# Narrow experts' products from loaded float32 weights on both column halves, and the sticks' sums in hi and lo parts

## The chip, the core and the metric

The kernel runs on one core of a Trainium2 chip. The metric is the device time of one execution in microseconds. In the names below PE is the matrix engine (TensorE), PEld its weight loads, DVE the vector engine, ACT the scalar engine, POOL GpSimd, and SP the sync engine, whose queue issues the large weight transfers.

## The reference

Two blocks of two layers each work on 256 tokens of width 1024 in float32. The first block has a retention layer, a dense layer, band attention and one layer with 8 experts, of which each token takes 2. The second block has two hybrid layers (stick-breaking attention, top-k attention, a gated recurrence) with an MLP behind each. The two places that matter here:

```python
# the experts: D_MODEL 1024, D_FF_EXPERT 3584, N_EXPERTS 8, TOP_K 2
for e in range(N_EXPERTS):
    y = y + gates[..., e:e + 1] * ((silu(xn @ w_gate[e]) * (xn @ w_up[e])) @ w_down[e])
...
# stick-breaking attention, six heads, blocks of 128 queries
log_1m = jnp.where(past, jax.nn.log_sigmoid(-z), 0.0)
later = lax.cumsum(log_1m, axis=3, reverse=True) - log_1m
a = jnp.exp(jnp.where(past, jax.nn.log_sigmoid(z) + later, NEG))
```

## The kernel before, in words

All weights are float32 in memory. PE multiplies "fp32r" operands, which keep fewer bits, so each float32 operand is cut in two: a high part (`whi`, a copy by ACT, L288) and a low part (`wlo`, the rest, by DVE, L289). A product is then three products of parts, hi·hi, lo·hi and hi·lo (`mm3`, L343 to L345).

The class `Stream` (L228 to L307) brings the weights. It holds a list of items in the order of use, each a tile of 128 partitions x 2048 float32, 1 MB. `fill` issues the transfer of the next items as long as a buffer is free; `_split` cuts the next half item into `whi` and `wlo` and frees the buffer when its second half is done; `get` hands out the parts that a product needs and lets `_split` run up to 5 half items (`HL`) ahead. There are 4 raw buffers (`RAW`), and 7 more (`widen`, pools raw3 and raw4) from the end of the attention layer to the last item of the last expert. SP issues the transfers in the order of the items, and each waits there for its buffer.

An expert is 42 items: for each of 14 blocks `j` of 256 hidden features two items of gate and up weights (`eu`) and one of down weights (`ed`). The eight experts are sorted by their load. Those in turns 0, 2, 3, 5 and 6 are wide (`WIDE`, L31): up to 128 slots, `mm3`. Those in turns 1, 4 and 7 are narrow: at most 64 slots. A narrow expert puts the high parts of its 64 tokens in columns 0 to 63 of the array and the low parts in columns 64 to 127 (`gather`, L977), so that two products, with `whi` (L1033) and with `wlo` (L1034), do all that is needed; a multiplication by `fold` (L1069), two identity matrices one above the other, adds both halves while it transposes.

In each block PE does the up products (`mm`), then the down products (`acc`) of the block before, then the transposes (`tp`); ACT and DVE do silu and the multiplication behind it (`split`, L1073, L1074). After the last block `acc` is cut into `yh` and `yl`, multiplied by the transposed one-hot matrix `ohT` (L1112) and added to `h` by DVE (L1114). The order on each engine comes from a scheduler, which is why work of two experts stands mixed where they meet.

`stick_breaking` (L1415) computes the sums over later keys as a product with a triangular matrix of ones (`c["later"]`), in float32, with four products of 128 columns for each of the two heads of a pair (L1443 to L1446); there are three pairs in each of two layers.

Of the kernel before, what the change touches and what calls it, by code (L numbers as in the profile page):

```python
# [23 lines left out]
KD = D // P  # L24
# [203 lines left out]
class Stream:  # L228


    def __init__(self, prog, plans, raw_bufs, hl_bufs, raw_pool, hl_pool):
        self.nc = prog.nc
        self.items, self.parts, self.first = [], [], []
        for ap, plan in plans:
            offs, _ = offsets(plan)
            for c, o in zip(plan, offs):
                self.first.append(len(self.parts))
                step = max(c.kt // 2, 1)
                self.parts += [(len(self.items), k, step) for k in range(0, c.kt, step)]
# [3 lines left out]
        self.free = {raw_pool: raw_bufs}  # L243
        self.base, self.extra = raw_pool, []
# [4 lines left out]
    def widen(self, pool, bufs, until):  # L249

        self.extra.append(pool)
        self.free[pool] = bufs
        self.last = next(i for i, it in enumerate(self.items) if it[1].key == until)
        self.fill()

    def fill(self, most=None):
        while self.n_raw < min(len(self.items), most or len(self.items)):
            pool = next((p for p in self.extra if self.n_raw <= self.last and self.free[p]), self.base)
            if not self.free[pool]:
                return  # L260
            ap, c, o = self.items[self.n_raw]
            f = c.kt * c.n
            t = pool.tile([P, 2048], F32, name="wraw")
            if c.key[0] in ("eu", "ed"):
                e = self.expert[c.key[1]] if c.key[1] else 0
                src = ap[e:e + 1] if isinstance(e, int) else ap[bass.ds(e, 1)]
                self.nc.sync.dma_start(t[:, :f], src[:, o:o + P * f].rearrange("o (p f) -> (o p) f", p=P))
            else:
                step = f if self.n_raw else f // 2
                for c0 in range(0, f, step):  # L270
                    self.nc.sync.dma_start(t[:, c0:c0 + step],
                                           bass.AP(tensor=ap.tensor, offset=ap.offset + o + c0, ap=[[f, P], [1, step]]))
            self.free[pool] -= 1
            self.raw[self.n_raw] = t, pool
            self.n_raw += 1

    def _split(self):
# [3 lines left out]
        t, pool = self.raw[i]  # L281
# [3 lines left out]
        for i0 in range(0, f, f // n):  # L285
            h, l = (x[:, i0:i0 + f // n] for x in (hi, lo))
            src = t[:, k * c.n + i0:k * c.n + i0 + f // n]
            self.nc.scalar.activation(h, src, AF.Copy)  # L288
            self.nc.vector.tensor_tensor(l, src, h.bitcast(F32), op=ALU.subtract)  # L289
        if k + nk == c.kt:  # L290
            self.free[pool] += 1
            del self.raw[i]
        self.hl[self.n_hl] = [x[:, :f].rearrange("p (k n) -> p k n", n=c.n) for x in (hi, lo)]
        self.n_hl += 1
        self.fill()

    def get(self, *keys):

        at = self.first[self.n_get]
# [3 lines left out]
        end = self.first[self.n_get]  # L303
        while self.n_hl < min(max(end, at + self.hl_bufs), len(self.parts)):
# [1328 lines left out]
```

## Time and profile before

| what | value |
| --- | --- |
| median of 3 runs | 2431.45 us (2431.17 to 2432.93) |
| the profiled execution's own time | 2430.9 us |
| its span, first to last instruction | 2429.1 us |
| busy: PE, PEld, DVE, ACT | 98%, 81%, 78%, 65% of the span |
| the eight experts | about 564 to 1536 us of the span |
| weights of the experts | 336 transfers of 1 MB |

The shares are means over stages with different limits. Matrix products overlap in PE's pipeline, so that a product's own duration is longer than the distance between the starts of two of them; PE's rate is read from starts. A plain float32 product stands in the trace as two records.

### The profile page before, as it was taken

The numbers are of one execution on the slowest core, as the hardware profiler recorded it, in microseconds if no ns is written. First come the engines' busy times: TensorE is split into PE (matmuls) and PEld (weight loads), VectorE is DVE, ScalarE is ACT, GpSimd is POOL, SyncE is SP. The second block draws the span as 40 slices with busy tenths as digits, with TensorE's granted clock in tenths as the row PEclk, the third lists the DMA queues.
The fourth block names the chain that finished last, engine by engine and source line by source line (L and its number), as shares of the span: only waits on it lengthen the run. The fifth ranks groups of instructions, "written<-read, shape, count | busy, mean of one in ns | idle before, by whom it ended". The sixth has DMA issues, their size and how long they took to land. (4 is left out here: it accounts for less than half of the span.)

```text
span 2429.1 us, 35661 instructions
## 1 busy us (share of the span) xinstructions
PE 2372.9 (98%) x13033; PEld 1968.2 (81%) x13033; DVE 1891.5 (78%) x3027; ACT 1568.7 (65%) x2609; POOL 60.5 (2%) x105
## 2 busy tenths in 40 slices
PE   8999999999999999999999999899999999999999
PEld 7978998888876787876788876698789889878898
DVE  6756567778989989899998899778775567877655
ACT  6446555667878777778777789645755554575554
POOL 0000000000000000000000000100000000100000
PEclk9999999999999999999999999899999999999999
DMA  7445555567989998999999999534345554434552
GB/s 289 169 161 209 190 191 191 203 239 283 368 327 399 360 366 330 356 356 413 345 366 345 367 359 381 148 134 160 137 165 203 188 168 145 169 128 173 191 191 105
DMA packets 88121, 605.20 MB, mean 249 GB/s; under 512 B 10456, under 2 KB 12128, under 8 KB 17024
## 3 DMA queue, kind: packets, MB, share of 16 engines
q1 hardware_dynamic: 85520, 593.39, 65.5%
q0 software_dynamic: 2416, 9.44, 1.8%
q8 instruction: 104, 1.70, 0.3%
q14 instruction: 81, 0.66, 0.1%
HBM read 601.74 MB, written 1.05 MB: 248 GB/s over the span
## 5 line engine op out<-in xcount | busy, mean ns | idle before, releaser
L289 DVE TENSOR_TENSOR wlo<-wraw,whi 128x512 fp32r<-128x512 f32 (+1 forms) x1656 | 1383.5, 876 | 369.6 <-ACT whi L288 351.7
L288 ACT ACTIVATE whi<-wraw 128x512 fp32r<-128x512 f32 (+1 forms) x1656 | 1204.1, 776 | 437.0 <-PE mm L344 191.6
L343 PE MATMUL mm<-xth,whi 128*128 128x256 f32 x1296 | 364.0, 281 | 0.0
L345 PE MATMUL mm<-xth,wlo 128*128 128x256 f32 x1296 | 361.7, 279 | 1.5 <-DVE wlo L289 1.5
L344 PE MATMUL mm<-xtl,whi 128*128 128x256 f32 x1296 | 361.8, 279 | 0.0
L344 PEld LDWEIGHTS mm<-xtl,whi 128*128 128x128 f32 x1296 | 245.5, 189 | 3.9 <-issue 2.1
L343 PEld LDWEIGHTS mm<-xth,whi 128*128 128x128 f32 x1296 | 243.5, 188 | 5.2 <-issue 3.0
L344 PE MATMUL acc<-wlo,hh 128*128 128x512 f32 x624 | 247.2, 396 | 0.0
L345 PE MATMUL acc<-whi,hl 128*128 128x512 f32 x624 | 246.6, 396 | 0.0
L345 PEld LDWEIGHTS mm<-xth,wlo 128*128 128x128 f32 x1296 | 243.6, 188 | 2.4 <-DVE wlo L289 1.7
L343 PE MATMUL acc<-whi,hh 128*128 128x512 f32 x624 | 235.3, 397 | 1.3 <-ACT hh L348 1.3
L343 PE MATMUL mm<-whi,xth 128*128 128x512 f32 (+2 forms) x592 | 231.3, 391 | 2.0 <-ACT whi L288 2.0
L344 PE MATMUL mm<-wlo,xth 128*128 128x512 f32 (+2 forms) x592 | 231.5, 391 | 0.3 <-DVE wlo L289 0.3
L345 PE MATMUL mm<-whi,xtl 128*128 128x512 f32 (+2 forms) x592 | 229.6, 388 | 0.5 <-DVE xtl L349 0.5
L343 PE MATMUL mm<-whi,xgh 128*128 128x512 f32 x560 | 224.9, 402 | 2.7 <-ACT whi L288 2.6
L344 PE MATMUL mm<-wlo,xgh 128*128 128x512 f32 x560 | 223.0, 398 | 3.1 <-DVE wlo L289 3.0
L345 PE MATMUL mm<-whi,xgl 128*128 128x512 f32 x560 | 221.4, 395 | 0.0
L1034 PE MATMUL mm<-wlo,xgh 128*128 128x512 f32 x336 | 143.3, 427 | 5.4 <-DVE wlo L289 4.5
L343 PEld LDWEIGHTS acc<-whi,hh 128*128 128x128 f32 x624 | 117.5, 188 | 28.9 <-ACT hh L348 3.2
L345 PEld LDWEIGHTS acc<-whi,hl 128*128 128x128 f32 x624 | 117.3, 188 | 28.2 <-DVE hl L349 0.5
L344 PEld LDWEIGHTS acc<-wlo,hh 128*128 128x128 f32 x624 | 117.4, 188 | 26.4 <-DVE wlo L289 0.3
L1033 PE MATMUL mm<-whi,xgh 128*128 128x512 f32 x336 | 134.2, 400 | 0.0
(394 smaller groups left out, 3098.0 us busy)
## 6 DMA issues: line engine op xcount, KB each, us to landing
wraw<-in_we_dram SPq DMA_DIRECT2D x336, 1024.0 KB, 6.1
wraw<-in_w_dram SPq DMA_DIRECT2D x218, 1024.0 KB, 4.8
wraw<-in_w_dram SPq DMA_DIRECT2D x4, 912.0 KB, 4.6
wraw<-in_w_dram SPq DMA_DIRECT2D x6, 512.0 KB, 3.6
bias<-in_rel_rows_dram POOLq DMA_DIRECT2D x4, 768.0 KB, 4.6
gain<-in_norm_ffn_dram POOLq DMA_DIRECT2D x2, 512.0 KB, 7.1
gn<-in_ret_gn_dram SPq DMA_DIRECT2D x4, 256.0 KB, 3.8
gain<-in_norm_ple_dram POOLq DMA_DIRECT2D x2, 512.0 KB, 5.9
```

What stands on the lines that cost most here:

```text
L288: self.nc.scalar.activation(h, src, AF.Copy)
L289: self.nc.vector.tensor_tensor(l, src, h.bitcast(F32), op=ALU.subtract)
L343: mm(out, l[0], r[0], start=start, stop=False)
L344: mm(out, l[0], r[1], start=False, stop=False)
L345: mm(out, l[1], r[0], start=False, stop=stop)
L1033: nc.tensor.matmul(out, x[0], wk[0], start=start, stop=False)
L1034: nc.tensor.matmul(out, x[0], wk[1], start=False, stop=stop)
```

## The change

In narrow experts the weights are no longer cut. `Stream.get` hands out the raw float32 tile itself, keeps its buffer until the next `get`, and only then frees it. Raw buffers are now parts of one tile for each pool, handed out from one list. The 64 tokens stay float32 (`xn`), and `halves` multiplies them as the array's stationary operand of 64 columns, once into partitions 0 to 63 with the left half of the weights' columns and once into 64 to 127 with the right half. The gate half and the up half of a block so land in the two partition halves of one bank with 256 columns, and the two halves of the model width in one bank with 512. Two plain transposes take the place of the fold; silu and the multiplication give the float32 `hn`, which isn't cut either. At the end one `yh` and one `yl` hold both halves, and the products with `ohT` take 64 rows each. Wide experts are as before. For the sticks' sums the triangle is stored as fp32r, the operand is cut in hi and lo parts, and each part takes one product of 384 columns and one of 128.

```diff
 class Stream:
+        self.plain = lambda c: c.key[0] in ("eu", "ed") and c.key[1] in plain
...
+    def room(self, pool, n, last):
+        t = pool.tile([P, n, 2048], F32, name="wraw")
+        self.last[id(t)] = last
+        self.free += [(t, k) for k in range(n)]
...
+    def release(self, i):
+        self.free.append(self.raw.pop(i))
+        self.fill()
...
     def get(self, *keys):
-        at = self.first[self.n_get]
+        for i in self.held:
+            self.release(i)
+        self.held = []
...
-        while self.n_hl < min(max(end, at + self.hl_bufs), len(self.parts)):
+        while self.n_hl < min(max(end, at + self.hl_bufs), len(self.parts)) \
+                and (self.n_hl < end or self.parts[self.n_hl][0] in self.raw):
             self._split()
+        if not self.plain(self.items[start][1]):
+            return [[x[:, k, :] for x in self.hl[i]] for i in range(at, end) for k in range(self.parts[i][2])]
+        self.held = list(range(start, self.n_get))
+        return [[t[:, a, k * c.n:(k + 1) * c.n]] for i in self.held
+                for (t, a), c in [(self.raw[i], self.items[i][1])] for k in range(c.kt)]
...
+    def halves(self, out, xs, ws, first, last):
+        m, width = None, out.shape[1]
+        for i, (x, (w,)) in enumerate(zip(xs, ws)):
+            for n in range(2):
+                before = [m] if m else []
+                m = self.nc.tensor.matmul(out[64 * n:64 * n + 64], x, w[:, n * width:(n + 1) * width],
+                                          start=first and i == 0, stop=last and i == len(xs) - 1)
+                self.after(m, before)
+        return m
...
+            def up(ps, k0, wu):
                 if wide[e]:
-                    self.mm3(out, x, wk, start, stop)
+                    for k in range(4):
+                        self.mm3(ps, [a[:, k0 + k, :] for a in xg], wu[k], k0 + k == 0, k0 + k == KD - 1)
                 else:
-                    nc.tensor.matmul(out, x[0], wk[0], start=start, stop=False)
-                    nc.tensor.matmul(out, x[0], wk[1], start=False, stop=stop)
+                    self.halves(ps[:, :256], [xg[:, k0 + k, :] for k in range(4)], wu, k0 == 0, k0 + 4 == KD)
...
+                if not wide[e]:
+                    if rows:
+                        ends.append(self.halves(acc[0], [hT[j][:, k, :] for j, k, _ in rows], [wk for *_, wk in rows],
+                                                 rows[0][:2] == (0, 0), rows[-1][:2] == (nj - 1, 1)))
+                    return
...
-                    for c in range(4):
-                        nc.tensor.matmul(tp[:, c], cp[:, c * P:(c + 1) * P], self.fold, start=True, stop=True)
+                    for k in range(2):
+                        self.after(nc.tensor.transpose(tp[:, k], cp[:, k * P:(k + 1) * P], self.ident), ends[-1:])
...
-                        nc.vector.tensor_tensor(sg, sg, tp[:, 2:], op=ALU.mult)
-                        self.split_psum(hh[:, :, :64], hh[:, :, 64:], sg)
+                        nc.vector.tensor_tensor(hT[j], sg, tp[:, :, 64:], op=ALU.mult)
...
-                nc.tensor.matmul(ps[:, 0:128], c["later"][:, 0], a[:, hh, 0:128], start=True, stop=True)
-                nc.tensor.matmul(ps[:, 128:256], c["later"][:, 0], a[:, hh, 128:256], start=True, stop=False)
-                nc.tensor.matmul(ps[:, 128:256], c["later"][:, 1], a[:, hh, 256:384], start=False, stop=True)
-                nc.tensor.matmul(ps[:, 256:384], c["later"][:, 0], a[:, hh, 256:384], start=True, stop=True)
+                parts = [pool.tile([P, 384], F32R, name="sah"), self.work.tile([P, 384], F32R, name="sal", tag="xs", bufs=3)]
+                self.split_psum(*parts, a[:, hh])
+                for x, w1, start, stop in ((0, 0, True, False), (0, 1, False, False), (1, 1, False, False), (1, 0, False, True)):
+                    if w1:
+                        nc.tensor.matmul(ps[:, 128:256], c["later"][:, 1], parts[x][:, 256:384], start=start, stop=stop)
+                    else:
+                        nc.tensor.matmul(ps[:, :384], c["later"][:, 0], parts[x], start=start, stop=stop)
```

How the order of instructions moves, at three places. First PE in a block of the narrow expert in turn 1. Before (`whi` and `wlo` are the cut weights, `xgh` the tokens' parts, `hh` the hidden features; "waits DVE" is the wait for a `wlo`, or in an `acc` row for `hh`):

```order
L1034 MATMUL mm<-wlo,xgh 128x512 [waits DVE_49]
L1033 MATMUL mm<-whi,xgh 128x512
L1034 MATMUL mm<-wlo,xgh 128x512
L1033 MATMUL mm<-whi,xgh 128x512 [waits Activation_49]
...
L1033 MATMUL acc<-whi,hh 128x512 [waits DVE_49]
L1034 MATMUL acc<-wlo,hh 128x512
...
L1069 MATMUL tp<-fold,cp 128x64 [waits Activation_49]
L1069 MATMUL tp<-fold,cp 128x64 x3
```

The same block now (`wraw` is the loaded tile; 64x256 and 64x512 are the outputs in one half of the array):

```order
L1048 MATMUL mm<-wraw,xn 64x256 [waits DMAHW2_49,PE_49]
L1048 MATMUL mm<-wraw,xn 64x256 x7
L1048 MATMUL mm<-wraw,xn 64x256 [waits DMAHW3_49]
L1048 MATMUL mm<-wraw,xn 64x256 x7
L1048 MATMUL acc<-wraw,hn 64x512 [waits DMAHW4_49,DVE_49]
L1048 MATMUL acc<-wraw,hn 64x512 x3
L1108 MATMUL tp<-ident,cp 128x128 [waits Activation_49]
L1108 MATMUL tp<-ident,cp 128x128
```

PE waited for DVE's parts of the weights; now it waits for each transfer itself.

Second, DVE where turn 1 (narrow) meets turn 2 (wide). Before (`sgn` and `hh` are the narrow expert's last hidden features, `yl` its output's low part, `h` the sum, the `wlo` rows from the second on belong to turn 2):

```order
L1074 TENSOR_TENSOR sgn<-sgn,tp 128x128 [waits Activation_49]
L289 TENSOR_TENSOR wlo<-wraw,whi 128x1024 [waits DMAHW7_49,Activation_49]
L349 TENSOR_TENSOR hh<-sgn,hh 128x2x64 [waits Activation_49]
L289 TENSOR_TENSOR wlo<-wraw,whi 128x1024 [waits Activation_49]
L289 TENSOR_TENSOR wlo<-wraw,whi 128x1024 [waits DMAHW0_49,Activation_49]
L349 TENSOR_TENSOR yl<-acc,yh 128x512 [waits Activation_49]
L289 TENSOR_TENSOR wlo<-wraw,whi 128x1024 [waits PE_49,Activation_49]
L1114 SCALAR_TENSOR_TENSOR h<-ps,in_turn,h 128x512 [waits PE_49] x2
```

Now:

```order
L1113 TENSOR_TENSOR hn<-sgn,tp 128x128 [waits DVE_49,Activation_49] x12
L368 TENSOR_TENSOR yl<-acc,yh 128x512 [waits Activation_49]
L1142 SCALAR_TENSOR_TENSOR h<-ps,in_turn,h 128x512 [waits PE_49]
L300 TENSOR_TENSOR wlo<-wraw,whi 128x1024 [waits DMAHW7_49,Activation_49]
L300 TENSOR_TENSOR wlo<-wraw,whi 128x1024 [waits Activation_49]
L1142 SCALAR_TENSOR_TENSOR h<-ps,in_turn,h 128x512 [waits PE_49] x3
L300 TENSOR_TENSOR wlo<-wraw,whi 128x1024 [waits DMAHW0_49,Activation_49]
```

The first low parts of the wide expert stood among the narrow expert's last steps; now they stand behind its output.

Third, SP's issues of expert weights in turn 1. Before, and below it now:

```order
L267 DMA wraw<-in_we_dram 128x2048 [waits DMAHW6_49,DVE_49]
L267 ISA
L267 DMA wraw<-in_we_dram 128x2048 [waits DMAHW7_49,DVE_49]
L267 ISA
L267 DMA wraw<-in_we_dram 128x2048 [waits DMAHW0_49,DVE_49]
```

```order
L275 DMA wraw<-in_we_dram 128x2048 [waits DMAHW6_49,DVE_49]
L275 ISA
L275 DMA wraw<-in_we_dram 128x2048 [waits DMAHW7_49,DVE_49]
L275 ISA
L275 DMA wraw<-in_we_dram 128x2048 [waits DMAHW0_49,PE_49]
```

From the item on whose buffer a narrow expert's weights held, the transfer waits for PE's products in place of DVE's low part.

## Rows read from the trace of the kernel before

**Rows 1.** The page's first line.
```profile
span 2429.1 us, 35661 instructions
```

**Rows 2.** Busy time by stage: from:to, length, engines (instructions), PEclk, DMA share, GB/s.
```profile
686.60:800.70 114.10, 101.53 (x465) 76.89 (x462) 106.73 (x119) 96.74 (x130) 0.00 (x0) 0.99 0.94 371
800.70:1054.00 253.30, 251.19 (x1122) 202.75 (x1123) 226.17 (x250) 187.92 (x235) 0.00 (x0) 0.99 0.93 352
1054.00:1166.00 112.00, 106.40 (x487) 76.26 (x485) 107.18 (x119) 96.38 (x130) 0.00 (x0) 1.00 0.98 391
1415.60:1533.10 117.50, 111.25 (x475) 73.67 (x472) 116.66 (x214) 107.15 (x222) 0.00 (x0) 0.99 0.84 330
1130.00:1166.00 36.00, 33.63 (x162) 24.24 (x160) 34.77 (x39) 32.16 (x44) 0.00 (x0) 1.00 1.01 416
```

**Rows 3.** Groups by line in turn 1, 686.6 to 800.7: busy, mean ns.
```profile
L289 DVE TENSOR_TENSOR wlo<-wraw,whi 128x1024 fp32r<-128x1024 f32 x84 | 98.9, 1220 | 2.5 <-ACT whi L288 1.8 <-PE tp L1069 0.7
L288 ACT ACTIVATE whi<-wraw 128x1024 fp32r<-128x1024 f32 x85 | 85.0, 1051 | 9.1 <-PE acc L1033 6.3 <-PE mm L1033 2.4 <-PE acc L345 0.3
```

**Rows 4.** Line L1034 (narrow, low parts): what PE sat idle for, us, times.
```profile
  DVE wlo L289: 61.4, 170
```

**Rows 5.** Timeline of PE in turn 1: start, length, line, idle before.
```profile
737.58 1.00 PE L1069 MATMUL tp<-fold,cp 128*128 128x64 f32 x8
...
738.70 0.39 PE L1033 MATMUL mm<-whi,xgh 128*128 128x512 f32 x1
738.93 0.40 PE L1034 MATMUL mm<-wlo,xgh 128*128 128x512 f32 x1
...
743.66 0.50 PE L1033 MATMUL acc<-whi,hh 128*128 128x512 f32 x1 [1.35 <-DVE hh L349]
```

**Rows 6.** Issues of weights by SP: start, length, count.
```profile
508.68 0.33 SPq L267 DMA_DIRECT2D wraw<-in_we_dram  x1
...
510.52 36.33 SPq L267 DMA_DIRECT2D wraw<-in_we_dram  x10
...
551.29 129.38 SPq L267 DMA_DIRECT2D wraw<-in_we_dram  x42
```

**Rows 7.** Transfers: count, KB each, median us from issue to landing.
```profile
wraw<-in_we_dram SPq DMA_DIRECT2D x336, 1024.0 KB, 6.1
```

**Rows 8.** Timeline of PE in the sticks' sums, float32 on the whole array.
```profile
1707.97 0.39 PE L1445 MATMUL sb<-sa,c_later 128*128 128x128 f32 x2
1708.19 0.39 PE L1446 MATMUL sb<-sa,c_later 128*128 128x128 f32 x2
```

**Rows 9.** Attention's float32 products on both column halves: the line's durations (ns), and a timeline.
```profile
L800 PE MATMUL po<-eT,v x96: 272/273/323, 472.0 to 527.6; 128*64 128x128 f32 x96
...
471.96 0.88 PE L800 MATMUL po<-eT,v 128*64 128x128 f32 x12
...
472.77 0.31 PEld L793 LDWEIGHTS pt<-ident,s 128*128 128x128 f32 x3 [0.17 <-issue]
```

**Rows 10.** Timeline where turn 1 meets turn 2.
```profile
802.18 0.60 ACT L348 ACTIVATE yh<-acc 128x512 fp32r<-128x512 f32 x1 [0.50 <-PE acc L1034]
...
803.04 0.68 DVE L349 TENSOR_TENSOR yl<-acc,yh 128x512 fp32r<-128x512 f32 x1
...
804.75 0.62 PE L1112 MATMUL ps<-yl,ohT 128*128 128x512 f32 x2
...
805.83 1.41 DVE L1114 SCALAR_TENSOR_TENSOR h<-ps,in_turn,h 128x512 f32<-128x512 f32 x2
```

**Rows 11.** Groups by line, 1000 to 1600 us: a wide block's steps behind the up products.
```profile
L1053 DVE TENSOR_TENSOR sg<-sg,mm 128x256 f32<-128x256 f32 x34 | 14.3, 420 | 2.9 <-ACT sg L1052 2.9
L1052 ACT ACTIVATE sg<-mm 128x256 f32<-128x256 f32 x34 | 13.1, 386 | 40.9 <-PE mm L345 40.9
```

**Rows 12.** The sticks: the step behind the sums (ns), and a stage with them (columns as rows 2).
```profile
L1447 DVE TENSOR_TENSOR zm<-zm,sb x12: 545/550/556, 1708.6 to 2162.7; 128x384 f32<-128x384 f32 x12
...
1680.00:1720.00 40.00, 38.62 (x215) 30.29 (x214) 31.86 (x77) 24.47 (x50) 0.00 (x0) 1.00 0.33 121
```

More of the change, by code (lines that the diff above doesn't have):

```diff
@@ L237, in __init__ @@
                 self.first.append(len(self.parts))
-                step = max(c.kt // 2, 1)
-                self.parts += [(len(self.items), k, step) for k in range(0, c.kt, step)]
+                if not self.plain(c):
+                    step = max(c.kt // 2, 1)
+                    self.parts += [(len(self.items), k, step) for k in range(0, c.kt, step)]
                 self.items.append((ap, c, o))
@@ L242, in __init__ @@
         self.first.append(len(self.parts))
-        self.free = {raw_pool: raw_bufs}
-        self.base, self.extra = raw_pool, []
+        self.free, self.last, self.held = [], {}, []
         self.hl_pool, self.hl_bufs = hl_pool, hl_bufs
@@ L247, in __init__, with widen @@
         self.n_raw = self.n_hl = self.n_get = 0
[L249 to L253, printed above, removed]
+        self.room(raw_pool, raw_bufs, len(self.items))
+    def room(self, pool, n, last):
+        t = pool.tile([P, n, 2048], F32, name="wraw")
+        self.last[id(t)] = last
+        self.free += [(t, k) for k in range(n)]
+    def widen(self, pool, n, until):
+        self.room(pool, n, 1 + next(i for i, it in enumerate(self.items) if it[1].key == until))
         self.fill()
@@ L257, in fill @@
         while self.n_raw < min(len(self.items), most or len(self.items)):
-            pool = next((p for p in self.extra if self.n_raw <= self.last and self.free[p]), self.base)
-            if not self.free[pool]:
+            place = next((p for p in self.free if self.n_raw < self.last[id(p[0])]), None)
+            if place is None:
                 return
+            self.free.remove(place)
+            t, at = place
             ap, c, o = self.items[self.n_raw]
             f = c.kt * c.n
-            t = pool.tile([P, 2048], F32, name="wraw")
             if c.key[0] in ("eu", "ed"):
@@ L280, in _split @@
         self.fill()
[L281 removed]
+        t, at = self.raw[i]
         f = nk * c.n
@@ L302, in get @@
             self.n_get += 1
-        end = self.first[self.n_get]
-        while self.n_hl < min(max(end, at + self.hl_bufs), len(self.parts)):
+        at, end = self.first[start], self.first[self.n_get]
+        self.fill()
+        while self.n_hl < min(max(end, at + self.hl_bufs), len(self.parts)) \
+                and (self.n_hl < end or self.parts[self.n_hl][0] in self.raw):
             self._split()
-        return [[x[:, k, :] for x in self.hl[i]] for i in range(at, end) for k in range(self.parts[i][2])]
+        if not self.plain(self.items[start][1]):
[3 more added lines that the diff above has]
+                for (t, a), c in [(self.raw[i], self.items[i][1])] for k in range(c.kt)]
 class Program:
@@ L522, in run @@
                                    (io["w2"], plan_second())], self.RAW, self.HL,
-                            raw_pool, hl_pool)
+                            raw_pool, hl_pool, [i for i in range(NE) if not WIDE[i]])
             self.h = self.keep.tile([P, NB, D], F32, name="h")
@@ L1086, in experts @@
                         split = None
-                    for k in range(4):
-                        product(ps, [a[:, k0 + k, :] for a in xg], wu[k],
-                                k0 + k == 0, k0 + k == KD - 1)
+                    up(ps, k0, wu)
                 rows = rows_of(j - 1) if 0 < j < nj - 1 else []
@@ L1170, in second_constants @@
         c = {}
-        for n in ("causal", "past_add", "past", "later", "rope", "levels"):
+        for n in ("causal", "past_add", "past", "rope", "levels"):
             c[n] = pool.tile(list(self.io[n].shape), I32 if n == "levels" else F32, name="c_" + n)
             self.nc.sync.dma_start(c[n], self.io[n])
+        ones = self.work.tile([P, 2, P], F32, name="ones", tag="xs", bufs=3)
+        self.nc.sync.dma_start(ones, self.io["later"])
+        c["later"] = pool.tile([P, 2, P], F32R, name="c_later")
+        self.nc.vector.tensor_copy(c["later"], ones)
         return c
```

99 lines of the change are left out of this document (56 added, 43 removed).

## The prediction, made before the changed kernel ran

> **What bounds the kernel now.** I began with the span [rows 1] and cut it into the experts' stages by the busy times per stretch [rows 2], since shares of the whole span mix stages with different limits. The narrow experts take 114.1 us (turn 1), 112.0 us (turn 4) and 117.5 us (turn 7, up to its last down product); two wide ones together 253.3 us, 126.6 us each. In the wide stages PE is busy for 251.2 of 253.3 us: they are bound by PE. In turn 1 DVE is busy for 106.7 of 114.1 us, 94%, and in turn 7 for 116.7 of 117.5 us, while PE has gaps of 12.6 and 6 us. The groups by line say with what: 84 low parts of 1220 ns are 98.9 us of DVE, the high parts 85.0 us of ACT [rows 3]. The waits before the products with low parts agree: 61.4 us over the three narrow experts [rows 4]. So narrow experts are bound by the cutting of weights, and the change takes that away whole.
>
> What is next must then be found. There are two candidates, both in these rows: the transfers, 42 items of 1 MB for an expert [rows 7], and PE with the new products.
>
> **The transfers.** With their engines full (share 1.01) they moved 416 GB/s in the stretch from 1130 us [rows 2]. An item of 1.0486 MB takes 2.52 us at that rate, an expert 105.9 us. But a narrow expert starts with buffers full. Up to 551 us 11 items had been issued and 42 more by 686.6 us [rows 6]; turn 0 used 42, so 11 of turn 1 were on their way or landed when it began. Left are 31 x 2.52 = 78.1 us. I add 3.7 us until the first buffer is freed, since its products stand mixed with 16 leftover products of turn 0 (16 x 0.23 us [rows 5]), 1.5 us for the last landing (an estimate, a quarter of the 6.1 us of rows 7, as its issue lies before) and 1.8 us of products behind it (below): 85.1 us.
>
> The Trainium skill, "DMA: Bandwidth & Descriptors", section "Specifications", gives a core about 358 GB/s from HBM. By that an expert would need 123 us and no narrow one could become shorter than it is. The measured 416 GB/s over 36 us [rows 2] decides against it; a milder form stays as a rival below.
>
> **PE's new products.** Float32 on the whole array: two records for 128 columns, the next pair 0.22 us later [rows 8], so 0.11 us a record; an fp32r product of 512 columns is 0.23 us behind the one before [rows 5]. Float32 thus costs four times as much per column. What pays for it is that the two column halves work side by side. The trace has such products: in attention 12 records of 128 columns, alternating between the halves, stand within 0.88 us, and the last one lasts 0.27 us, so 11 steps take 0.61 us, 0.055 us each, half of 0.11 [rows 8, 9]. With the number of columns a record costs 0.11 us at 256 and 0.22 us at 512. A block has 16 up products, 32 records, 3.55 us, and 4 down products, 8 records, 1.78 us. The fold of 1.00 us [rows 5], 8 records, becomes two transposes of a record each, 0.25 us. Twice a block the array changes between halves and whole; behind the products on halves a weight load stood 0.17 us without cause [rows 9], so 0.3 us. That is 5.88 us, 82.3 us for 14 blocks. At the end silu and the multiplication lie open, at most 0.39 + 0.42 us as in a wide block [rows 11], and the last down products, 0.9 us: 84.0 us.
>
> The Trainium skill, "TensorEngine Tiling (Array Packing)", section "Key Properties", says that changing the tiling mode drains the engine. This is the rule that speaks against the change. The 0.17 us agree with it in kind; the sum above has them, and a larger price is a rival.
>
> Both limits lie near 85 us. They overlap, not add: PE eats the 11 items of lead, then waits for transfers in the last blocks. I take 85 us.
>
> **Silu, copies, `hn`.** The copy of 256 columns, silu and one multiplication remain on ACT and DVE, both now nearly idle, under the 3.55 us of the next up products: nothing. If that cover went, they would cost at most the 0.39 + 0.42 us of the wide form [rows 11] in 14 blocks, 11 us.
>
> **Where a narrow expert meets a wide one.** Before, the wide expert's low parts were made ahead. Now DVE has them behind `yl` and a sum into `h`, and ACT has the high parts behind `yh` (the second place of the order). So behind the last down product come `yh` 0.60, `yl` 0.68, products with `ohT` 0.62, one sum 0.70, one low part 1.22 [rows 3, 10], with four hand-overs of 0.3 us (`yh` ends at 802.78, `yl` starts at 803.04) 5.0 us. In the first wide block only four half items are cut ahead, and ACT goes on only after that block's silu and `hh`: silu 0.39, multiplication 0.42, transposes 0.25, `hh` 0.39 (a copy of the same size as silu), a high part 1.05 and a low part 1.22 [rows 3, 11] are 3.7 us; with hand-overs I take 4 us. Both hold for turns 1 and 4. What waits behind these instructions on DVE and ACT is the wide expert's own cutting, and PE for it.
>
> **The sum for the experts.** To the point where PE runs through again a narrow expert takes 85 + 5 + 4 = 94 us. Before, that point was the stage's length plus 3.7 us of leftover products (16 x 0.23). Turn 1: 117.8 - 94 = 23.8. Turn 4: 115.7 - 94 = 21.7. Turn 7 has no wide expert behind it: 117.5 - 85 = 32.5, less 3 us because all four sums into `h` now stand at the end: 29.5. Together 75.0 us.
>
> Does the lead come back before turns 4 and 7? Wide experts use an item in 126.6 / 42 = 3.01 us, transfers bring one in 2.52 us. Over 84 items this is 41 us, 16 items, more than the 11 buffers: yes. For wide experts that start with empty buffers I take off 4.5 us in all, a high and a low part (2.27 us) for each of turns 2 and 5; it lies between 0 and twice that.
>
> **The sticks.** For each of 12 heads four products of 0.22 us become 2 x 0.17 + 2 x 0.06 us: 5.2 us of PE less. Added for each are a copy of 384 columns (about 0.5 us, from 0.60 for 512) and a subtraction (0.55 us, as the step of the same size in rows 12) in a chain. In such a stage PE is busy for 38.6 of 40 us with other products and ACT for 24.5 [rows 12], so the chain is mostly covered. Bounds: 5 us gained to 12 us lost; I take 2 us gained, near the busy PE.
>
> In the profiled execution, 2430.9 us with 2429.1 us of span, this is 75.0 - 4.5 + 2 = 72.5 us: 2358.4 us. The median is 0.55 us above that execution; I forecast **2359 us**.
>
> **Rivals.**
>
> *The transfers don't hold 416 GB/s in the long run.* Over whole stages they moved 352 to 391 GB/s [rows 2]. For it: turn 1's share of 0.94 at 371 is not far from full. Against it: in wide stages PE asks for no more. At 371 GB/s an item takes 2.83 us; turn 1 is 31 x 2.83 + 6.2 + 9 = 103, 15 us won; the wide experts refill 84 x 0.18 / 2.83 = 5 items, so turn 4 takes 37 x 2.83 + 15 = 120 and turn 7 about 114: 4 lost, 3 won. That is some 14 us, 2417 us.
>
> *Changing the array's mode costs more.* At 1 us each instead of 0.15 a block takes 7.6 us, an expert 108: with 9 us behind it turns 1 and 4 win nothing, turn 7 some 7 us, 2426 us. At 0.5 us a block is 6.6 us, an expert 94, 9 us more than forecast in each of three, 2386 us. Against it: the 0.17 us.
>
> *The halves don't overlap at 256 and 512 columns, the other side.* The overlap is seen at 128 columns alone. One after the other a block is 32 x 0.11 x 2 + 8 x 0.22 x 2 + 0.5 = 11 us, an expert 156, 42 us more than now, and with the meetings above some 140 us lost: 2570 us. It decides from a block of 8 us, about what one takes now (114.1 / 14). Against it: nothing in rows 9 depends on the length of a stream, and a longer one hides the weight loads better.
>
> *Nothing moves, because another wait sits right behind DVE's.* For it: ACT has 96.7 of 114.1 us of work in turn 1. Against it: most of that is the 85.0 us of high parts, which go too.
>
> **How the numbers follow.** My forecast, with the transfers and PE near 85 us, gets 0.80; its own range is 2343 to 2376: below, each narrow expert is 5 us shorter (boundaries better covered); above, the lead isn't quite full and the sticks lose. A sagging rate gets 0.07, a dear change of mode 0.07 (half of it near 2386), no overlap 0.04, nothing moved 0.02. The range for 8 in 10 reaches to the milder form of the mode's price and of the rate: 2338 to 2398 us. Two runs of this kernel can be told apart from about 0.2%, 5 us. Faster by more: 0.94, the forecast and the first two rivals; within it 0.02; slower 0.04.
>
> **What would show it.** Right: no cut weights in turns 1, 4 and 7; records of 64 output rows some 0.11 us (up) and 0.22 us (down) apart; blocks of 5.9 us at first and, in the last blocks, PE idle on `wraw` transfers; a transfer share near 1.0 at about 415 GB/s through turn 1 and the wide experts after it; a gap of some 5 us at the start of turns 2 and 5. Wrong: blocks over 8 us, transfers that stay below 390 GB/s with their share at 1, or turn 4 much longer than turn 1.

## The result and the profile after

| | median, us | range | runs |
|---|---|---|---|
| before | 2431.31 | 2430.47 to 2432.93 | 4 |
| changed | 2403.78 | 2400.02 to 2407.41 | 4 |

The ratio is 0.988, with a 95% interval of 0.987 to 0.990. The kernel became 27.5 us faster where 72.5 were forecast; 2404 us lies outside the forecast's range of 2338 to 2398. The profiled execution of the changed kernel took 2407.41 us, 3.6 us above the median, so differences of stages below are good to some 4 us.

The page's first line:

```profile
span 2405.6 us, 35418 instructions
```

Busy time by stage in the changed kernel (columns as in [rows 2]). The first four rows answer to rows of it: turn 1, turns 2 and 3, turn 4 and turn 7. The others are short stretches that the text comes to.

```profile
690.70:782.50 91.80, 88.53 (x609) 45.90 (x608) 8.56 (x21) 10.85 (x31) 0.00 (x0) 1.00 0.89 366
782.50:1046.60 264.10, 254.79 (x1109) 201.76 (x1109) 225.79 (x247) 186.35 (x232) 0.00 (x0) 0.97 0.92 370
1046.60:1140.80 94.20, 91.68 (x641) 48.31 (x640) 11.12 (x26) 13.45 (x35) 0.00 (x0) 1.00 0.91 370
1399.60:1491.70 92.10, 88.58 (x609) 45.91 (x608) 8.55 (x21) 10.85 (x31) 0.00 (x0) 1.00 0.95 387
1491.70:1523.50 31.80, 5.81 (x25) 4.06 (x25) 13.42 (x21) 9.43 (x20) 5.26 (x10) 0.58 0.80 206
690.00:695.00 5.00, 5.00 (x25) 3.45 (x24) 1.12 (x2) 1.17 (x3) 0.00 (x0) 1.00 0.00 0
695.00:700.00 5.00, 5.00 (x24) 2.28 (x24) 2.33 (x4) 0.41 (x1) 0.00 (x0) 1.00 0.21 49
720.00:760.00 40.00, 40.00 (x298) 21.07 (x296) 2.02 (x7) 4.63 (x14) 0.00 (x0) 1.00 1.01 421
770.00:800.00 30.00, 23.82 (x107) 13.33 (x108) 8.71 (x11) 5.43 (x8) 0.00 (x0) 0.89 0.51 199
```

In turn 1 DVE fell from 106.7 to 8.6 us and ACT from 96.7 to 10.9 us: the cutting is gone, as the change says. The stages are 18 to 25 us shorter than in [rows 2], but turns 2 and 3 grew from 253.3 to 264.1 us, with PE idle for 9 us of them. Behind turn 7 there are 31.8 us in which PE works for 5.8. They end with the first product of the side branch (`self.ple`), which is the next work of PE behind the experts. In the kernel before, from that stage's end (1533.1) to the branch's first product (1542.8), it was 9.7 us:

```profile
1542.80 0.77 PE L343 MATMUL mm<-whi,xth 128*128 128x512 f32 x1
```

The span as a whole, cut where narrow experts begin and at that first product (1542.8 before, 1523.5 after):

| from, to | before | after | change | forecast |
|---|---|---|---|---|
| start to turn 1 | 686.6 | 690.7 | +4.1 | 0 |
| turns 1 to 3 | 367.4 | 355.9 | -11.5 | -21.5 |
| turns 4 to 6 | 361.6 | 353.0 | -8.6 | -19.4 |
| turn 7 to the branch's first product | 127.2 | 123.9 | -3.3 | -29.5 |
| from there to the end | 886.3 | 882.1 | -4.2 | -2.0 |

Some 10 us are missing in each group of a narrow expert with two wide ones, and 26 us at turn 7. The 4.1 us ahead of turn 1 are partly this execution: turn 1 began between 686.9 and 689.1 us in all other runs below with the new narrow experts.

**What happened behind turn 1.** Rows of SP's issues in the changed kernel, then of what its queue waited for from 757 to 800 us (total, times, longest), then of ACT:

```profile
760.08 2.82 SPq L275 DMA_DIRECT2D wraw<-in_we_dram  x2
787.47 0.33 SPq L275 DMA_DIRECT2D wraw<-in_we_dram  x1
```

```profile
SPq L275 <- DMA wraw<-in_we_dram: 30.6, 5, 19.3
SPq L275 <- DVE wlo L300: 8.5, 2, 5.1
```

```profile
793.74 2.00 ACT L299 ACTIVATE whi<-wraw 128x1024 fp32r<-128x1024 f32 x2 [8.72 <-DMA wraw<-in_we_dram]
```

From 762.90 to 787.47 us, for 24.6 us, SP issued no transfer. In its written order two transfers into buffers of the wide expert's first items stand ahead of those into buffers of turn 1 (the `ISA` rows between them are left out):

```order
L275 DMA wraw<-in_we_dram 128x2048 [waits DMAHW7_49,DMAHW0_49,DVE_49]
...
L275 DMA wraw<-in_we_dram 128x2048 [waits DMAHW1_49,DMAHW0_49,DVE_49]
...
L275 DMA wraw<-in_we_dram 128x2048 [waits DMAHW2_49,PE_49]
```

The code gives a wide item's buffer back when it writes down its cut, and a narrow expert writes down cuts of the next expert's items early (`get` calls `_split` ahead). On the chip such an item is the last of the queue: its transfer lands only at turn 1's end (19.3 us of waiting), and its low part is made behind `yl` (5.1 us more). In all that time PE frees buffers of turn 1, and the transfers for them stand behind. The transfers fell to 199 GB/s from 770 to 800 us, turn 2 began with empty buffers, and ACT waited 8.72 us for the next item.

The waits cost more than their own length, because TensorE's clock fell behind them. From 800 to 810 us the transfers ran full again, but PE waited 0.77, 1.51 and 0.76 us in it and was granted 0.67 of its clock:

```profile
800.00:810.00 10.00, 6.96 (x18) 4.81 (x18) 7.24 (x8) 6.76 (x8) 0.00 (x0) 0.67 1.01 427
```

```profile
805.12 0.63 PE L364 MATMUL mm<-whi,xw 128*128 128x512 f32 x1
805.55 0.63 PE L362 MATMUL mm<-whi,xw 128*128 128x512 f32 x1
```

Twelve products in a row stand 0.43 us apart there, at the lower of the two levels (1.2 GHz); at the upper one (2.4 GHz) they stand 0.23 us apart [rows 5].

**What happened behind turn 7.** DVE in the kernel before:

```profile
1539.52 2.65 DVE L415 TENSOR_TENSOR xs<-h,gain 128x512 f32<-128x512 f32 x4 [2.11 <-DVEq L1136]
...
1546.98 1.23 DVE L1152 TENSOR_TENSOR gm<-gm,gf 128x1024 f32<-128x1024 f32 x1 [1.19 <-DMA gm<-in_norm_mix_dram]
```

DVE in the changed kernel, PE for it, and the longest piece of the chain that ended last:

```profile
1510.11 1.22 DVE L1201 TENSOR_TENSOR gm<-gm,gf 128x1024 f32<-128x1024 f32 x1 [9.53 <-DMA gm<-in_norm_mix_dram]
...
1520.79 0.29 DVE L1226 CAST c_later<-ones 128x256 fp32r<-128x256 f32 x1 [5.84 <-DMA ones<-in_later_dram]
1521.12 1.29 DVE L434 TENSOR_TENSOR xs<-h,gain 128x512 f32<-128x512 f32 x2
```

```profile
1514.49 1.94 PE L402 MATMUL tp<-ident,xs 128*128 128x128 f32 x8 [18.65 <-DVE xs L434]
1521.86 1.97 PE L402 MATMUL tp<-ident,xs 128*128 128x128 f32 x8 [5.43 <-DVE xs L434]
```

```profile
1504.11 16.56 DMA ones<-in_later_dram
```

The new constant `ones` takes a buffer of the tag `xs`, which the branch's first instructions need. With it DVE's order changed: the product of two gains, which stood behind all four `xs` before, now stands ahead of them and waits 9.53 us, and the constant's cast stands between them and waits 5.84 us. The transfer of `ones` took 16.56 us; five transfers of the branch's weights and five of other constants stand just ahead of it in SP's queue.

### The profile page after: what moved, and what is told of

It is laid out like the page before. It is cut to its first block, busy times and chain, and to the rows that moved or that the text cites. A ratio compares the mean times of both kernels' runs of the same rounds, so it can differ in the third digit from the quotient of the medians.

```text
span 2405.6 us, 35418 instructions
## 1 busy us (share of the span) xinstructions
PE 2327.7 (97%) x13405; PEld 1876.1 (78%) x13405; DVE 1595.3 (66%) x2659; ACT 1306.7 (54%) x2236; POOL 60.1 (2%) x105
## 5 line engine op out<-in xcount | busy, mean ns | idle before, releaser
L300 DVE TENSOR_TENSOR wlo<-wraw,whi 128x512 fp32r<-128x512 f32 (+2 forms) x1320 | 1081.6, 855 | 372.8 <-ACT whi L299 355.2
L299 ACT ACTIVATE whi<-wraw 128x512 fp32r<-128x512 f32 (+2 forms) x1320 | 942.0, 760 | 441.1 <-PE mm L363 194.8
L1048 PE MATMUL mm<-wraw,xn 128*64 128x256 f32 x1344 | 161.4, 383 | 2.7 <-DMA wraw<-in_we_dram 2.7
L1113 DVE TENSOR_TENSOR hn<-sgn,tp 128x128 f32<-128x128 f32 x42 | 12.1, 288 | 221.7 <-ACT sgn L1112 221.7
L362 PE MATMUL mm<-whi,xgh 128*128 128x512 f32 x336 | 136.7, 407 | 4.5 <-ACT whi L299 4.5
L1048 PEld LDWEIGHTS mm<-wraw,xn 128*64 128x64 f32 x1344 | 93.8, 137 | 56.4 <-issue 10.4
L363 PE MATMUL mm<-wlo,xgh 128*128 128x512 f32 x336 | 135.8, 404 | 1.8 <-DVE wlo L300 1.8
```

Source lines behind the costliest of these rows:

```text
L362: mm(out, l[0], r[0], start=start, stop=False)
L363: mm(out, l[0], r[1], start=False, stop=False)
L1048: m = self.nc.tensor.matmul(out[64 * n:64 * n + 64], x, w[:, n * width:(n + 1) * width], start=first and i == 0, stop=last and i == len(xs ...
L1113: nc.vector.tensor_tensor(hT[j], sg, tp[:, :, 64:], op=ALU.mult)
```

## The experiments

Theory A: SP's queue was blocked at the two meetings of a narrow with a wide expert. Theory B: behind turn 7 the cast and the gains' product stood in DVE's way. The rivals: to A, the transfers' gap is hidden by full buffers; to B, PE waits behind turn 7 for the branch's weights in any case.

**Buffers given back later.** Cuts stay where they were; only the buffers' return moves to the wide expert's first request.

```
+        if k + nk == c.kt and owe:
+            self.owed.append(i)
-        if k + nk == c.kt:
+        elif k + nk == c.kt:
             self.release(i)
...
+        if not ahead:                 # ahead: the request is a narrow expert's
+            for i in self.owed:
+                self.release(i)
```

> Only SyncE's order changes: the buffers of wide items that are cut ahead from a narrow expert are given back when the wide expert begins, not at the cut. Theory (a transfer that waits for VectorE's late cut stands at the head of SyncE's queue, from 762.9 to 787.5 us in the changed kernel's trace, and some nine transfers whose buffers TensorE has long freed stand behind it; the same at the next meeting of a narrow with a wide expert): the gap in the transfers goes, the wide expert runs through from its first product on, about 15 us at each of two meetings: 30 us less than the changed kernel (20 to 40), about 2374 us. Rival (TensorE's gaps after the meeting come from VectorE's cuts, which stand behind yl and h in either kernel, and from the lower clock; the transfers' gap is hidden by buffers): 0 to 5 us less, 2399 to 2404 us.

Measured: 2375.6 us (2372.4 to 2377.5), ratio to before 0.9765 (0.9752 to 0.9778), 28 us less than the changed kernel. Theory A holds. From 770 to 800 us the transfers, which had 199 GB/s, now run full, and SP's longest wait there is 2.0 us. From 800 to 810 us the clock is 1.00, with 47 matrix instructions in place of 18. The second pair of wide experts (turns 5 and 6) is shown in the changed kernel and below it in this run:

```profile
770.00:800.00 30.00, 26.19 (x116) 15.32 (x117) 14.52 (x18) 11.90 (x16) 0.00 (x0) 0.89 1.01 421
800.00:810.00 10.00, 10.00 (x47) 8.19 (x46) 8.97 (x10) 6.46 (x8) 0.00 (x0) 1.00 1.02 424
782.50:1036.60 254.10, 250.20 (x1111) 199.52 (x1110) 225.65 (x247) 186.07 (x232) 0.00 (x0) 0.99 0.96 380
```

```profile
1140.80:1399.60 258.80, 250.20 (x1104) 199.93 (x1102) 223.05 (x238) 183.09 (x227) 0.00 (x0) 0.98 0.95 377
...
1130.60:1379.70 249.10, 247.05 (x1102) 198.15 (x1102) 222.54 (x238) 182.93 (x227) 0.00 (x0) 0.99 0.97 384
```

```profile
SPq L275 <- DMA wraw<-in_we_dram: 32.5, 17, 2.0
```

Turns 2 and 3 take 254.1 us, 10 less. Not all of the 28 us is from the meetings: these gave some 20 us (the wide pairs 264.1 to 254.1 and 258.8 to 249.1), and a part of that is the clock that no longer falls so long. Behind turn 7, where SP gives buffers back in the same way, the branch's first product came 22.7 instead of 31.8 us after the last down product.

**Nothing cut ahead.** A narrow expert makes no cuts for the next one: `while not self.plain(...) and ...` ahead of the loop in `get`.

> A narrow expert cuts nothing ahead for the wide expert behind it. The order of the transfers becomes that of the run with the late return, so the theory of SyncE's queue expects the same gain, 20 to 40 us; the first cut of the wide expert starts only at its first request, so up to 4 us per meeting are lost against that run (0 to 8 us in all). If the cutting ahead itself were what the changed kernel lacks, this would be the slowest of the two by 10 us or more.

Measured: 2373.3 us (2372.0 to 2376.9), ratio 0.9764 (0.9750 to 0.9777), as the run before. The cutting ahead is worth nothing that can be measured; what it did to SP's order cost 28 to 30 us.

**The cast late.** `ones` is loaded into a part of a tile of the last stage and cast ahead of the sticks' inputs.

```
-        ones = self.work.tile([P, 2, P], F32, name="ones", tag="xs", bufs=3)
...
-        self.nc.vector.tensor_copy(c["later"], ones)
...
+            ones = rT[:, 8].rearrange("p (k s) -> p k s", s=P)
+            self.nc.sync.dma_start(ones, self.io["later"])
...
+            self.nc.vector.tensor_copy(c["later"], ones)
             q, k = self.stick_inputs(l, sb, row)
```

> The constant of the sticks' sums is loaded into a tile of the last stage and cast just ahead of the sticks, not among the constants ahead of the side branch. Theory (VectorE stands 5.84 us in the cast of that constant, whose transfer is the last of the constants behind a full queue, and 9.53 us in the product of the two gains that now stands ahead of the branch's first instruction): TensorE's idle 18.65 + 5.43 us after the last expert falls to about the 4.8 us of the kernel before, 19 us less than the changed kernel (14 to 22), about 2385 us; if only the cast goes and the gains' product keeps its place, 5 to 8 us less. Rival (TensorE waits there for the weights of the branch, which come late whatever VectorE does; ScalarE waits 5.98 us for one): at most 5 us less.

Measured: 2393.5 us (2391.2 to 2396.4), ratio 0.9841 (0.9827 to 0.9854): 10 us less than the changed kernel, between theory and rival. DVE had all four `xs` ahead of the gains' product again, and the branch's first product came 12.6 us behind the last down product instead of 31.8. But of these 19 us some 8 were given back at once: from there to the end it took 889.9 us instead of 882.1. The 20 us behind that product, in the changed kernel and then in this run:

```profile
1523.50:1543.50 20.00, 20.00 (x85) 16.11 (x84) 12.49 (x21) 10.64 (x20) 0.00 (x0) 0.90 0.30 107
```

```profile
1502.40:1522.40 20.00, 15.35 (x56) 11.36 (x54) 7.52 (x12) 6.89 (x13) 2.52 (x5) 0.86 0.85 186
```

PE idles for 4.7 of them. The rows of DVE and PE say for what:

```profile
1508.08 1.22 DVE L1201 TENSOR_TENSOR gm<-gm,gf 128x1024 f32<-128x1024 f32 x1 [5.67 <-DMA gm<-in_norm_mix_dram]
```

```profile
1509.96 0.50 PE L364 MATMUL mm<-whi,xtl 128*128 128x512 f32 x1 [3.12 <-DVE xtl L368]
1521.82 0.73 PE L362 MATMUL mm<-whi,xth 128*128 128x512 f32 x2 [1.26 <-ACT whi L299]
```

The larger part, 3.1 us, is DVE's order once more: the gains' product now stands behind the four `xs` but ahead of the last two `xtl`, waits there 5.67 us for the transfer of `gm`, and PE waits for `xtl`. Behind that wait products stand 0.43 us apart again (1511.65 to 1514.21 us). Only 1.3 us are a wait for weights of the branch. So the theory was right that DVE's order held the branch up, but the gain was smaller since the next wait in that order stood right behind; of the rival's late weights this run shows little.

**Both.** 

> Late return of the buffers and late cast together. Theory: the two places are 800 us apart and add up, 30 + 19 = 49 us less than the changed kernel (34 to 60), about 2355 us, near the forecast of 2359. Rival (either gain is eaten at the next limit, the transfers of the last narrow expert and of the branch): less than 25 us.

Measured: 2371.6 us (2367.8 to 2375.7), ratio 0.9746 (0.9733 to 0.9760), 32 us less, where 49 were expected and 38 would be the sum of the two runs. They don't add up, because giving buffers back late had already shortened the way to the branch's first product from 31.8 to 22.7 us. With both it is 16.1 us, so the late cast wins 6.6 us there and not 19, and from that product to the end it takes 884.5 us instead of 880.8.

**All three.** Nothing cut ahead, the cast late, and the gains' product written behind `self.ple(...)`.

> No cutting ahead from narrow experts, the constant cast just ahead of the sticks, and the product of the two gains written behind the side branch; VectorE then has the branch's four first instructions right behind the jump at the experts' end, with neither cuts nor the product ahead of them. Theory: from the last down product to the branch's first product 11 us instead of the 20.6 of the run without cutting ahead, the rest as there: 2373.3 - 9 = 2364 us (2358 to 2369). Rival (the branch is bound by its weights' transfers, which then come late): as the run with late return and late cast, 2371 us.

Measured: 2372.6 us (2366.7 to 2374.0), ratio 0.9751 (0.9737 to 0.9765): the rival's number, no better than the last two. The step did what it should: the branch's first product came 12.4 us behind the last down product (1465.9 to 1478.3 us), not 20.6 as with nothing cut ahead alone. And most of these 8.2 us went again: from there to the end it took 887.2 us, where that run took 881.6. Here it is the branch's weights: ACT waits 3.27 us for one, and PE idles for 3.2 of its first 20 us behind that:

```profile
1373.80:1465.90 92.10, 88.50 (x609) 45.91 (x608) 8.56 (x21) 10.85 (x31) 0.00 (x0) 1.00 0.95 386
1478.30:1498.30 20.00, 16.83 (x79) 13.48 (x78) 15.01 (x24) 11.33 (x23) 4.42 (x6) 0.99 0.99 244
```

```profile
1494.37 0.63 ACT L299 ACTIVATE whi<-wraw 128x512 fp32r<-128x512 f32 x1 [3.27 <-DMA wraw<-in_w_dram]
```

**Half the bytes.** The same kernel, but the narrow experts of turns 4 and 7 load half of each item. The other half of the buffer keeps what it held before, so the output is not the layer's; PE's work is the same.

```
+                s = src[:, o:o + P * f].rearrange("o (p f) -> (o p) f", p=P)
+                g = f // 2 if self.plain(c) and c.key[1] > 1 else f
+                self.nc.sync.dma_start(t[:, at, :g], s[:, :g])
```

> As the run with all three repairs (nothing cut ahead, cast late, gains' product late), but the narrow experts of turns 4 and 7 load only the first half of each item's columns; their other half is what the buffer held before. TensorE's work is unchanged. Theory (a narrow expert's last blocks, and the side branch behind turn 7, are bound by transfers that were not issued while all buffers stood full at the expert's start): turns 4 and 7 become 4 us shorter each, 89 instead of 93 us, with blocks of 5.7 us to the end, and the branch's first 20 us lose their 3 to 5 us of idle: 2372.6 - 13 = 2360 us (2354 to 2364). Rival (transfers are hidden; the stage's length is TensorE's): 2370 us or more.

Measured: 2355.0 us (2351.8 to 2356.1), ratio 0.9678 (0.9664 to 0.9691), 17.6 us less than with all three repairs; between the profiled executions it is 11.1 us (a span of 2354.4 against 2365.5). Turn 7 takes 88.1 us, and the branch's first 20 us are full:

```profile
1371.70:1459.80 88.10, 87.32 (x609) 45.69 (x608) 14.70 (x31) 16.17 (x41) 0.00 (x0) 1.00 0.74 260
1471.60:1491.60 20.00, 20.00 (x91) 16.38 (x90) 13.21 (x21) 11.30 (x21) 2.88 (x6) 0.95 0.86 184
```

Turn 7 wins 4.0 us, the wide pair behind turn 4 3.4 us (247.8 to 244.4), and the stretch from the branch's first product to the end 4.4 us (887.2 to 882.8). So transfers bind the end of turn 7 and the start of what follows a narrow expert. Turn 4 itself did not become shorter (94.1 us, 93.9 without this edit), against the expectation. PE waits for no transfer in it in either run; products that gather the tokens of turns 5 and 6 stand in its last block.

**The sums.** Three runs: the changed kernel with the old sums, the kernel before with the new ones, and that with the cast late.

> The changed kernel with the sticks' sums as before (four float32 products, the constant loaded as it is, no cast). VectorE's order behind the last expert is that of the run with the late cast. Theory (the sums themselves are worth about 4 us, read from 882.1 against 886.3 us from the branch's first product to the end): 4 us slower than the run with the late cast, 2393.5 + 4 = 2397 us, and so faster than the changed kernel by some 6 us, since the cast and its wait go. Rival (hi and lo sums cost time, in their chain of copy, subtraction and products): 2389 us or less.

> The kernel before with the new sums and their cast constant alone; the experts as before. Theory: the sums win 4 us, and the cast's wait and the gains' product, which now stands ahead of two of the branch's four first instructions on VectorE, lose some 5 to 10 us: 2431 + 1 to 6, 2432 to 2437 us. If the constant's transfer hurts only where the transfers' queue is full behind a narrow expert that is bound by it, 2427 us.

> The kernel before with the new sums, and their constant loaded and cast just ahead of the sticks. Theory (the sums win 4 to 5 us by themselves; the 3 us that the sums alone lost were the cast's place): 2432 - 4 = 2428 us (2425 to 2430). Rival (the sums' chain is not covered, so they win nothing): 2432 us or more.

Measured: 2398.7 us (2398.1 to 2400.4), ratio 0.9864 (0.9849 to 0.9879); 2435.4 us (2432.2 to 2438.0), ratio 1.0013 (1.0004 to 1.0022); 2429.3 us (2426.6 to 2432.6), ratio 0.9990 (0.9981 to 0.9999). All three are as expected. The first is 5.2 us above the run with the cast late, which has the same order of DVE behind turn 7; the third is 2.7 us below the kernel before. So the sums win 3 to 5 us, and the place of their constant, with the order that it makes on DVE, cost the kernel before 6 us (2435.4 against 2429.3). In the second run the gains' product stood behind two of the four `xs` like this:

```profile
1543.38 1.28 DVE L415 TENSOR_TENSOR xs<-h,gain 128x512 f32<-128x512 f32 x2
1550.65 1.23 DVE L1152 TENSOR_TENSOR gm<-gm,gf 128x1024 f32<-128x1024 f32 x1 [5.99 <-DMA gm<-in_norm_mix_dram]
```

**The price of a half.** In `halves`, first the loops are exchanged, so that the four up products of an item go to one half and then four to the other (in the down products two and two):

```
-        for i, (x, (w,)) in enumerate(zip(xs, ws)):
-            for n in range(2):
+        for n in range(2):
+            for i, (x, (w,)) in enumerate(zip(xs, ws)):
```

> In the narrow experts all products of one column half are issued before those of the other, instead of one by one in turn; nothing else changes. Theory (two products overlap when neighbours go to different halves): without the alternation a float32 record of 256 columns takes 0.22 us instead of 0.11, a block 11 us instead of 5.7, and each of three narrow experts 156 us instead of 92: about 190 us more, 2595 us. Rival (a product on half of the array costs half by itself, in any order): 2404 us, as the changed kernel.

Then all products go to one half, with outputs in two places of rows 0 to 63:

```
-    m = self.nc.tensor.matmul(out[64 * n:64 * n + 64], x, ...
+    o = out[n][:64] if isinstance(out, list) else out[:64, n * width:(n + 1) * width]
+    m = self.nc.tensor.matmul(o, x, ...
```

> All products of the narrow experts go to the same half of the array (columns 0 to 63); their two results stand in two places of rows 0 to 63 and are put together by the copies behind them, one copy more per block. Theory (a float32 record of 64 output rows takes 0.21 us per 256 columns by itself, and two overlap on different halves): a block takes 32 x 0.21 + 8 x 0.43 + 0.5 = 10.7 us instead of 5.7, a narrow expert some 155 us, the kernel about 190 us more than the changed one, 2594 us. Rival (half of the array costs half by itself, and the run with grouped products lost only their hand-overs): blocks of 5.7 to 6.7 us, 2404 to 2440 us.

Measured: grouped 2437.9 us (2434.1 to 2438.9), ratio 1.0021 (1.0011 to 1.0030), 34 us more than the changed kernel. A block is 6.72 us, from one block's transposes to the next one's:

```profile
719.84 0.44 PE L1108 MATMUL tp<-ident,cp 128*128 128x128 f32 x2
...
726.56 0.44 PE L1108 MATMUL tp<-ident,cp 128*128 128x128 f32 x2
```

Both expectations missed: it costs 18% of a block, neither nothing nor as much again.

One half: 2566.0 us (2560.8 to 2566.3), ratio 1.0550 (1.0534 to 1.0566), with this block:

```profile
743.51 0.44 PE L1111 MATMUL tp<-ident,cp 128*128 128x128 f32 x2
743.88 7.12 PE L1050 MATMUL mm<-wraw,xn 128*64 128x256 f32 x32
750.84 3.60 PE L1050 MATMUL acc<-wraw,hn 128*64 128x512 f32 x8
754.36 0.44 PE L1111 MATMUL tp<-ident,cp 128*128 128x128 f32 x2
```

A block is 10.85 us, near the theory's 10.7: 0.22 us a record of 256 columns (6.96 / 32) and 0.44 us of 512 (3.52 / 8), twice the times with both halves. Halves do overlap, and that is shown now, not inferred. The time is 28 us below the expected 2594: the three stages grew by 67, 71 and 67 us, but transfers had that time to fill the buffers, and the wide pairs behind shrank to 247.9 and 244.8 us, the way to the branch to 13.5 us. The same bargain seen from its other side.

## Why the prediction was wrong

**Right: what bounded the kernel, and the new products.** The cut weights are gone, and with them DVE's and ACT's load. The block came out at 5.69 us, forecast 5.88:

```profile
724.79 3.67 PE L1048 MATMUL mm<-wraw,xn 128*64 128x256 f32 x32
728.29 1.89 PE L1048 MATMUL acc<-wraw,hn 128*64 128x512 f32 x8
730.11 0.44 PE L1108 MATMUL tp<-ident,cp 128*128 128x128 f32 x2
730.48 3.67 PE L1048 MATMUL mm<-wraw,xn 128*64 128x256 f32 x32
```

The rivals of a dear change of mode and of halves without overlap fell with this block. So did the sagging rate: 421 GB/s at a share of 1.01 from 720 to 760 us. Silu and `hn` cost nothing but for the last block, where PE waits 0.75 us for `hn`. The last blocks wait for `wraw`, as foretold; one of these rows:

```profile
767.45 1.95 PE L1048 MATMUL mm<-wraw,xn 128*64 128x256 f32 x16 [0.44 <-DMA wraw<-in_we_dram]
```

**Mis-sized: "3.7 us until the first buffer is freed".** The transfers stood at 0 GB/s from 690 to 695 us and at 49 GB/s up to 700: with all buffers full, the first freed one came when the first item's products, mixed with turn 0's last products and its sums into `h`, were through at 698 us, 7.4 us into the turn. The stage took 91.8 us, not 85.1; the late first buffer is 3.7 of these 6.7 us. In the rest, which is not split further here, is a slow start of the transfers, 334 GB/s from 700 to 705 us:

```profile
700.00:705.00 5.00, 5.00 (x44) 3.07 (x42) 1.37 (x3) 0.66 (x2) 0.00 (x0) 1.00 0.90 334
```

**Mis-sized the other way: 5.0 and 4 us where narrow meets wide.** With SP's queue free (buffers given back later) the pair of wide experts took 254.1 us; the forecast's terms give 253.3 - 3.7 + 9 + 2.25 = 260.9. In that run the two errors cancel, by luck: turns 1 to 3 were forecast at 345.9 us and took 347.5 (689.1 to 1036.6), turns 4 to 6 at 342.2 and took 343.1.

**The first step that failed: "For wide experts that start with empty buffers I take off 4.5 us in all", between 0 and 9.** The buffers were empty as said, but the sum took for granted that SP issues as buffers come free. It issues in its written order, and the change put two transfers early in it whose buffers come free last. That cost 20 us at two meetings and up to 9 us behind turn 7; undoing it alone gave 28. The part of SP's order that stands ahead of the prediction ends before these two transfers, and it is read there for what stands in a row, not for when each row's wait ends. The fall of the clock behind the waits is in no term of the sum either.

**The second: "Turn 7 has no wide expert behind it", 29.5 us.** 3.3 came. Of the 26 missing, 7 are the stage's length (92.1 instead of 85), and 19 lie between the last down product and the branch. There the `ones` of the sticks changed the order on DVE. I had costed the sticks by their 12 heads and their constant at nothing, without naming what stands behind its cast on DVE. The runs put it as follows: with nothing cut ahead, late cast and late product that way is 12.4 us instead of 31.8, the forecast's 9.7 + 3; but from there to the end it takes 887.2 us, not the changed kernel's 882.1, and 3.2 us of that are a wait for the branch's weights. With the late cast alone it takes 889.9 us, and 3.1 us of that are the gains' product. The forecast had no term for what a narrow expert's empty buffers cost the branch.

What is left with all three repairs fits this: the profiled execution's span of 2365.5 us is 8.9 us above the forecast's 2356.6 (2429.1 - 72.5). Of this 6.8 us lie between turn 7's start and the branch's first product (104.5 us, forecast 97.7), all of it in the stage itself, and 2.9 us behind that product (887.2, forecast 884.3); what stands ahead of turn 7 is together 0.8 us under the forecast.

**The sticks: 2 us forecast, 3 to 5 found** without their constant's place. (PE's saving is 12 x 0.42 = 5.0 us by the prediction's own terms, not 5.2.)

**Misread, without harm to the sum: "61.4 us over the three narrow experts".** These waits of line L1034 are mostly those of PEld, the weight loads, which have the same line: 56.3 us in 153 waits. PE itself waited there 5.1 us in 17, and all its gaps in the three stages are 24.4 us [rows 2]. That cutting bounded the narrow experts rests on DVE's 94% and on the stages' fall. The prediction's 123 us for an expert also leave out the 11 items of lead that its own sum counts; the sum did not use them.

What stays open: some of the 4.1 us ahead of turn 1, and what makes the clock differ from one execution to the next. All three repairs have a median only 0.7 us below nothing cut ahead alone, though their profiled execution is 6.0 us shorter (2365.5 against 2371.5 us of span). That execution is one of the two quickest of five (2366.7 and 2367.3 us, at a mean granted clock of 0.995 and 0.996; the others took 2372.6 to 2374.0 us at 0.993), so the 6.0 us are not shown to be the repairs'. Both of these versions and the one with late return and late cast beat the changed kernel and the one before; the last is at 2371.6 us, 32 us under the one, 60 under the other and 13 above the forecast.

## What to carry to other kernels

An order of transfers is a queue: ask of each one in it not when it is issued but when its buffer comes free, and whether those behind it are ready sooner. A stage that becomes faster than its transfers hands on empty buffers, so part of what it wins is lost at the start of the next one; count both together. And a small constant costs what stands behind its wait on an engine that works in order, not its own 0.29 us.

## What the runs showed of the hardware that was not expected

- Products on two halves of the array overlap almost as well when four neighbours (two in the down products) go to one half before the other's turn: 6.72 us a block against 5.69 in turn and 10.85 on one half alone. Alternating one by one was worth 1 us a block, using both halves 5.
- Transfers of weights held 419 to 424 GB/s at a share of 1.00 to 1.02 where the buffers were free, from 710 to 780 us in the changed kernel.
- A transfer of 128 KB (`ones`) issued behind five of weights and five of constants took 16.56 us to land; that of the gains `gm`, 512 KB, 9.1 us.
- Short waits cost TensorE its clock: from 800 to 810 us the granted clock was 0.67 in the changed kernel behind waits of 0.77, 1.51 and 0.76 us, and 1.00 in the run without SP's gap. Twelve products at the lower level took 2.4 us longer than at the upper one.
